# A transformer layer on one core: its first loads in halves, and the last of seven products added on in PSUM

## The chip, the cores and the metric

The kernel runs on one core of a Trainium2 chip. The core has a matrix engine (TensorE, PE in the profile; PEld is its weight load), a vector engine (VectorE, DVE), an activation engine (ScalarE, ACT), GpSimd (POOL), and SyncE (SP), whose queue issues all of this kernel's DMAs to 16 DMA engines. Products are accumulated in eight PSUM banks; everything else works in SBUF. The metric is the device time of one execution in microseconds; a median over runs is given.

## The reference, cut to what matters

One layer over 1024 rows of width 1024, in fp32:

```python
h = rmsnorm(x, g_mix_pre)
proj = h @ w_in                     # q, k, v of two groups of heads, and 8 forget-gate logits
y = concat(rmsnorm(forgetting_attention(...)), rmsnorm(chunked_attention(...)))
x = x + rmsnorm(y @ w_out, g_mix_post)
x = x + rmsnorm(memory_cross_attention(rmsnorm(x, g_mem_pre), ...), g_mem_post)
h = rmsnorm(x, g_ff_pre)
y = square(relu(h @ w_ff1)) @ w_ff2 # hidden width 4096
x = x + rmsnorm(y, g_ff_post)
```

## The kernel before

Every fp32 product is made as three products of rounded parts: an operand is split into a high part (a copy rounded to the type that PE takes) and a low part (the operand less its high part), and `mm3` (lines 191 to 195) multiplies high by high, high by low and low by high into one bank. So each operand costs a copy and a subtraction before PE can use it: mostly the copy on ACT and the subtraction on DVE.

**The start.** x comes transposed from the host (`xT`), 512 rows at a time (a half `th`), in four pairs of 128-row chunks of the width (`load_pair`, 512 KB each). The first work on PE are the values of the first 512 rows, block by block of 128 rows: group 1 (the chunked heads, 256 columns, weights `w_v1`) and group 0 (the forgetting heads with the gate's logits, 264 columns, `w_v0`). `value_weights` loads `w_v1` in two blocks of four chunks and `w_v0` in blocks of three, three and two; `value_split` splits them. `gained(kc)` multiplies a chunk of x by its gain and splits it (ACT writes `hT_hi`, DVE `hT_lo`). `square(kc)` squares a chunk on ACT and adds it up on DVE; the sum goes through PE (`ssx`) and POOL (a power of -0.5) to become the inverse norm of each row, `rcols[0]`. The other half's inverse norm, `rcols[1]`, comes from the rows of x themselves: four loads (`row`), four squares with a running sum on ACT (`row_squares`), POOL. While they wait for that, 30 transposes of the identity (`warm`) keep PE at work.

The order on every engine in this part, in the middle of the feed-forward layer and at the end is the order in which the code issues the instructions (`tc.manual_schedule()`); each engine works through its own in that order, and SP's queue too. Only the attention between them is ordered by a planner (`Flow`). A tile's `bufs` say how many buffers its tag has; a new tile waits until the one whose buffer it takes has been used for the last time. In the first stage PE goes through the eight chunks with four banks at once (96 products), then `ssx`, then the group-0 values of block 0 and block 1 (24 products each), then a transpose that spreads the inverse norms over the partitions (`rr`), and further values.

**The feed-forward layer.** Both matrix products are done by seven products of half-size blocks with added and subtracted operands (Strassen's scheme in Winograd's form). The first product's outputs `u`, `g` and `s` are combined on DVE (`sums`, lines 1974 to 1984) and written to DRAM (`put`). The second product takes its seven products in this order, each in eight steps of 24 products:

```python
order = ((0, "B11"), (1, "B21"), (4, "T2"), (3, "T1"), (5, "T3"), (6, "B22"), (2, "T4"))
```

`fetch(s)` loads the operands of step `s`, and `prepare(s)` (lines 1876 to 1905) makes the weight operand and splits both. Two sets of four banks are used: `X` and `Y`. B11 starts X; T2 and T3 are added on in the same banks; B21 and T1 start Y, B22 is added on to T1. `gather` (line 2044) takes a product's banks out into the output rows `yc`. Before, T4 starts fresh banks, and `gather` subtracts them from what T3 left.

**The end.** The last three steps of T4 are done block by block (`tp`), so that each block's rows can be finished beside the next: `gather`, `squares` (square with sum on ACT, gain on DVE), `inverse` (POOL), `finish` (DVE adds the residual, SP writes the result).

Of the kernel before, what the change touches and what calls it, by code (L numbers as in the profile page):

```python
# [14 lines left out]
F32 = mybir.dt.float32  # L15
# [7 lines left out]
P = 128  # L23
# [112 lines left out]
def build(ctx, tc, nc, out, t):  # L136
# [150 lines left out]
    def value_weights(g, raws=None, only=None):  # L287

        n = 264 if g == 0 else 256
        src = t["w_v0"] if g == 0 else t["w_v1"]  # L290
        raws = [] if raws is None else raws
        for i, (a, b) in enumerate(((0, 3), (3, 6), (6, 8)) if g == 0 else ((0, 4), (4, 8))):
            if only in (None, i):
                raw = wp.tile([P, b - a, n], F32, tag="wraw", bufs=3, name=f"wrawv{g}{a}")
                nc.sync.dma_start(raw, src[:, a:b, :])
                raws.append(raw)
        return raws

    def value_split(g, raw, i, pieces=1):
        k, shape = raw.shape[1], list(raw.shape)  # L300
        if g == 1:
            wh, wl = (wp.tile(shape, F32R, tag=x, bufs=2, name=f"{x}v{i}") for x in ("whi", "wlo"))
        else:
            wh, wl = (u4(f"{x}v0{i}", shape) for x in ("whi", "wlo"))
        n = k // pieces
        for j in range(0, k, n):
            nc.scalar.activation(wh[:, j:j + n, :], raw[:, j:j + n, :], AF.Copy)
            nc.vector.tensor_sub(wl[:, j:j + n, :], raw[:, j:j + n, :], f(wh[:, j:j + n, :]))
        return [(wh[:, j, :], wl[:, j, :]) for j in range(k)]
# [1060 lines left out]
    with tc.manual_schedule():  # L1370
        xT = {0: [load_pair(0, 0)], 1: []}
        gmix = const.tile([P, KC], F32, name="gmix")
        nc.sync.dma_start(gmix, t["g_mix_pre"])
        raw1 = value_weights(1, None, 0)
        xT[0] += [load_pair(0, 1), load_pair(0, 2)]
        value_weights(1, raw1, 1)
        xT[0].append(load_pair(0, 3))
        raw0 = value_weights(0, None, 0)
# [5 lines left out]
        def gained(kc):  # L1384

            x, g, dh = xT[0][kc // 2][:, kc % 2, :], gmix[:, kc:kc + 1], hT[0].hi(kc)
            nc.scalar.activation(dh, x, AF.Copy, scale=g)
            nc.vector.scalar_tensor_tensor(hT[0].lo(kc), x, g, f(dh), op0=ALU.mult, op1=ALU.subtract)
# [11 lines left out]
        for kc in (0, 1):  # L1400
            gained(kc)
        w1 += value_split(1, raw1[0], 0, 2)
# [26 lines left out]
        w0 += value_split(0, raw0[1], 1)  # L1429
        nc.vector.tensor_scalar(rcols[0], ps, EPS, None, op0=ALU.add)  # L1430
        nc.gpsimd.tensor_tensor(rcols[0], rcols[0], mhalf[:, 0:4], op=ALU.pow)
        w0 += value_split(0, raw0[2], 2)

        def row(b):
            xr.append(p1.tile([P, D], F32, tag="sp", bufs=5, name=f"x{b}"))
            nc.sync.dma_start(xr[-1], t["x"][b * P:(b + 1) * P, :])
# [439 lines left out]
    def prepare(s):  # L1876

        n, k = steps[s]
        name = order[n][1]
        ra = rows_a.pop(s)  # L1880
        if s % 3 == 2 or s == len(steps) - 1:
            ah, al, bh, bl = [u4(f"{m}{s}", (P, D)) for m in ("ah", "al", "bh", "bl")]
        else:
            ah, al = [wp.tile([P, D], F32R, tag=m, bufs=2, name=f"{m}f{s}") for m in ("whi", "wlo")]
            bh, bl = [pws[s % 3].tile([P, D], F32R, tag=f"v{s % 3}{m}", bufs=1, name=f"v{m}f{s}")
                          for m in ("hi", "lo")]
        rb = rows_b.pop(s)[0] if name not in ("B11", "T1") else None
# [10 lines left out]
        nc.scalar.activation(ah, ra, AF.Copy)  # L1898
        nc.scalar.activation(bh, rb, AF.Copy)
        nc.vector.tensor_sub(al, ra, f(ah))  # L1900
        nc.vector.tensor_sub(bl, rb, f(bh))
        if name == "B11":
            t1[k] = u4(f"t1_{k}", (P, D), F32)
            nc.vector.tensor_sub(t1[k], r12, rb)
        ops[s] = (ah, al, bh, bl)

    with manual:
# [79 lines left out]
        sums()  # L1987


        pfs.close()  # L1990
        yc, ssf = {}, {}

        def squares(b, nh, apart=False):

            y = yc[b][:, nh * HT:(nh + 1) * HT]
            if b not in ssf:
                ssf[b] = small.tile([P, 2], F32, tag="ssf", bufs=8, name=f"sf{b}")
            junk = pw.tile([P, HT], BF16, tag="sd", bufs=1, name=f"jf{b}{nh}")
            nc.scalar.activation(junk, y, AF.Square, scale=1.0 / 32.0, accum_out=ssf[b][:, nh:nh + 1])  # L1999
            g = yg[b, nh] = u4(f"yg{b}{nh}", (P, HT), F32) if apart else y  # L2000
            nc.vector.tensor_tensor(g, y, gfin[:, nh * HT:(nh + 1) * HT], op=ALU.mult)
# [42 lines left out]
        def gather(n, tp, ps):  # L2044
# [10 lines left out]
            elif n == 4:  # L2055
                nc.scalar.activation(half(hi, 0), ps, AF.Copy)
                nc.vector.tensor_add(half(hi, 1), ps, half(hi, 1))
            elif n == 5:
                nc.vector.tensor_add(half(lo, 1), ps, half(lo, 1))
            else:  # L2060
                nc.vector.tensor_sub(half(hi, 0), half(hi, 0), ps)
# [19 lines left out]
        for n in range(7):  # L2081
            if n in (0, 6):
# [5 lines left out]
            for k in range(NK - tail):  # L2088
                s = n * NK + k
                if s + 2 < len(steps):  # L2090
                    prepare(s + 2)
                if s + 4 == len(steps):
# [5 lines left out]
                multiply(banks, range(4), [s], n in (2, 4, 5))  # L2098
# [10 lines left out]
        for tp in range(4):  # L2109
            multiply(X, [tp], range(len(steps) - 3, len(steps)), False)  # L2110
# [9 lines left out]
def _layout(i):  # L2120
# [10 lines left out]
    def rows(w):  # L2131
        return a(w.reshape(KC, P, -1).transpose(1, 0, 2))
# [10 lines left out]
        "w_v0": rows(np.concatenate([fv[:, :256], fg], 1)),  # L2143
        "w_v1": rows(cv[:, :256]),
# [29 lines left out]
```

## Time and profile before

| what | value |
|---|---|
| median of 3 runs | 1483.99 us (1483.71 to 1484.88) |
| profiled execution | 1484.06 us, its span 1482.3 us |
| PE busy | 1466.0 us, 99% of the span |
| DVE busy | 948.6 us, 64% |
| ACT busy | 797.3 us, 54% |
| POOL busy | 391.3 us, 26% |
| moved by DMA | 220.67 MB, mean 149 GB/s |
| granted PE clock, mean | 0.999 |

The profile is that of one execution. The span runs from the first to the last recorded instruction; the time of the execution is a little longer. A row of a timeline gives start, duration, engine, line of the kernel, operation, output and inputs, shapes, how many instructions are merged (x2), and in brackets how long the engine had been idle before and what released it. Line numbers are those of the kernel before. A wait list names who waited, for whom, and how long in total, how often, and the longest. Rows of PE overlap, as products are pipelined: the distance between two starts is what one costs.

### The profile page before, as it was taken

The numbers are of one execution on the slowest core, as the hardware profiler recorded it, in microseconds if no ns is written. First come the engines' busy times: TensorE is split into PE (matmuls) and PEld (weight loads), VectorE is DVE, ScalarE is ACT, GpSimd is POOL, SyncE is SP. The second block draws the span as 40 slices with busy tenths as digits, with TensorE's granted clock in tenths as the row PEclk, the third lists the DMA queues.
The fourth block names the chain that finished last, engine by engine and source line by source line (L and its number), as shares of the span: only waits on it lengthen the run. The fifth ranks groups of instructions, "written<-read, shape, count | busy, mean of one in ns | idle before, by whom it ended". The sixth has DMA issues, their size and how long they took to land. (4 is left out here: it accounts for less than half of the span.)

```text
span 1482.3 us, 21601 instructions
## 1 busy us (share of the span) xinstructions
PE 1466.0 (99%) x7606; PEld 1250.3 (84%) x7606; DVE 948.6 (64%) x1644; ACT 797.3 (54%) x1417; POOL 391.3 (26%) x613
## 2 busy tenths in 40 slices
PE   8999999999999999999999999999999999999998
PEld 8989888888889988888888887888888888888886
DVE  6777667565576835974384687675444665656577
ACT  6567567465567835553353455555555453443542
POOL 0144355353344200531041413432222000000021
PEclk9999999999999999999999999999999999999999
DMA  7133322522315552461251447674445785445565
GB/s 271 48 87 79 82 67 70 150 67 60 79 58 149 176 178 85 154 202 58 89 182 43 153 146 241 235 243 148 155 150 170 250 346 178 142 139 202 178 247 199
DMA packets 83484, 220.67 MB, mean 149 GB/s; under 512 B 10008, under 2 KB 14112, under 8 KB 83376
## 3 DMA queue, kind: packets, MB, share of 16 engines
q1 hardware_dynamic: 83376, 219.30, 44.6%
q8 instruction: 60, 0.98, 0.3%
q14 instruction: 48, 0.39, 0.1%
HBM read 159.96 MB, written 50.91 MB: 142 GB/s over the span
## 5 line engine op out<-in xcount | busy, mean ns | idle before, releaser
L700 DVE TENSOR_TENSOR pl<-ptr,ph 128x512 fp32r<-128x512 f32 (+1 forms) x152 | 92.2, 616 | 39.5 <-ACT ph L703 34.8
L1898 ACT ACTIVATE whif<-ra 128x1024 fp32r<-128x1024 f32 x37 | 39.2, 1061 | 122.1 <-PE fy L194 62.6
L1900 DVE TENSOR_TENSOR wlof<-ra,whif 128x1024 fp32r<-128x1024 f32 x37 | 45.3, 1225 | 91.2 <-ACT whif L1898 91.2
L703 ACT ACTIVATE ph<-ptr 128x512 fp32r<-128x512 f32 (+1 forms) x152 | 79.1, 539 | 39.4 <-PE ptr L694 32.9
L2014 POOL TENSOR_SCALAR rf<-sf 128x1 f32<-128x1 f32 x8 | 8.2, 1028 | 326.6 <-ACT jf L1999 326.3
L731 PE MATMUL pv<-ph,vs 128*128 128x256 f32 x304 | 79.6, 286 | 0.0
L732 PE MATMUL pv<-pl,vs 128*128 128x256 f32 x304 | 78.6, 283 | 0.3 <-DVE pl L700 0.3
L193 PE MATMUL fx<-vhif,whif 128*128 128x512 f32 x168 | 65.4, 389 | 0.0
L194 PE MATMUL fx<-vlof,whif 128*128 128x512 f32 x168 | 65.4, 389 | 0.0
L195 PE MATMUL fx<-vhif,wlof 128*128 128x512 f32 x168 | 65.4, 389 | 0.0
L732 PEld LDWEIGHTS pv<-pl,vs 128*128 128x128 f32 x304 | 57.6, 189 | 4.6 <-POOL pl L689 0.5
L731 PEld LDWEIGHTS pv<-ph,vs 128*128 128x128 f32 x304 | 57.3, 189 | 4.1
L1788 POOL TENSOR_TENSOR sc<-wf,wf 128x512 f32<-128x512 f32 x14 | 20.1, 1437 | 144.0 <-DMA wf<-in_w_ff 89.3
L193 PE MATMUL k<-hT_hi,whik 128*128 128x512 f32 x128 | 52.5, 411 | 0.0
L193 PE MATMUL mq<-h2T_hi,whimq 128*128 128x512 f32 x128 | 51.5, 403 | 0.0
L193 PE MATMUL q<-hT_hi,whiq 128*128 128x512 f32 x128 | 50.9, 398 | 0.0
L193 PE MATMUL ym<-whimo,oT_hi 128*128 128x512 f32 x128 | 50.3, 394 | 0.1
L194 PE MATMUL k<-hT_lo,whik 128*128 128x512 f32 x128 | 50.2, 393 | 0.0
L193 PE MATMUL yw<-whiwo,yT_hi 128*128 128x512 f32 x128 | 50.2, 392 | 0.0
L195 PE MATMUL k<-hT_hi,wlok 128*128 128x512 f32 x128 | 50.1, 392 | 0.0
L194 PE MATMUL q<-hT_lo,whiq 128*128 128x512 f32 x128 | 50.1, 391 | 0.0
L195 PE MATMUL mq<-h2T_hi,wlomq 128*128 128x512 f32 x128 | 50.1, 391 | 0.0
(606 smaller groups left out, 5027.1 us busy)
## 6 DMA issues: line engine op xcount, KB each, us to landing
ra<-gd SPq DMA_DIRECT2D x56, 512.0 KB, 3.9
wg<-in_w_ff SPq DMA_DIRECT2D x56, 512.0 KB, 5.9
wf<-in_w_ff SPq DMA_DIRECT2D x38, 512.0 KB, 4.0
gd<-s SPq DMA_DIRECT2D x48, 256.0 KB, 2.1
wrawmq<-in_w_mq SPq DMA_DIRECT2D x16, 512.0 KB, 3.8
wrawmo<-in_w_mo SPq DMA_DIRECT2D x16, 512.0 KB, 3.8
gd<-u SPq DMA_DIRECT2D x32, 256.0 KB, 2.1
gd<-g SPq DMA_DIRECT2D x25, 256.0 KB, 2.5
```

The source lines that it names most:

```text
L193: nc.tensor.matmul(ps, lh, rh, start=start, stop=False, skip_group_check=more)
L194: nc.tensor.matmul(ps, lh, rl, start=False, stop=False, skip_group_check=more)
L195: nc.tensor.matmul(ps, ll, rh, start=False, stop=stop, skip_group_check=more)
L700: flow.put("V", at, 0.7, lambda: nc.vector.tensor_sub(pl[:, live, :], tr[:, live, :], f(ph[:, live, :])), done)
L703: flow.put("S", flow.end, 0.6, lambda ph=ph, tr=tr, live=live: nc.scalar.activation(ph[:, live, :], tr[:, live, :], AF.Copy), split)
L731: nc.tensor.matmul(pv, v, ph[:, hs, :], start=c == 0 and half == 0, stop=False)
L732: nc.tensor.matmul(pv, v, pl[:, hs, :], start=False, stop=c + 1 == len(steps) and half == 1)
L1788: eng.tensor_sub(sc[:, k1], r0[:, k0], r1[:, k0])
L1898: nc.scalar.activation(ah, ra, AF.Copy)
L1900: nc.vector.tensor_sub(al, ra, f(ah))
L2014: nc.gpsimd.tensor_scalar(r, ssf[b][:, 0:1], ssf[b][:, 1:2], EPS, op0=ALU.add, op1=ALU.add)
```

## The change

It has three parts.

1. The start. A tiny activation (`early`) is issued first on ACT. The first pair of x and the first block of `w_v1` are loaded in two halves each, in the order x, gmix, weights, x, weights. `w_v0` and `w_v1` are laid out by block in DRAM, so that a block is contiguous. The high part of the first block of `w_v1` is copied by POOL instead of ACT, and its low part goes ahead of the low parts of x on DVE. There are 20 warm-up transposes instead of 30. The second block of `w_v0` gets a buffer of another tag (`bias`) and is loaded and split sooner; two of the four rows of x are loaded ahead of the third block; the values of group 0, block 0 are issued before `ssx`; all four `row_squares` go ahead of `value_leave`.
2. Between the two feed-forward products: `prepare(2)` to `prepare(4)` are issued ahead of the last `sums()`, with its four writes to DRAM, instead of behind it.
3. The end: T4's operand is made with the opposite sign, and its products are added on in X, in the banks in which T3 ended. The copies of half of X after T3 and the four subtractions of `gather` go; `squares` reads the bank itself, on ACT and DVE.

```diff
-    def load_pair(th, p):
+    def load_pair(th, p, halves=False):
...
-        nc.sync.dma_start(xt, t["xT"][th, p])
-        return xt
+        if not halves:
+            nc.sync.dma_start(xt, t["xT"][th, p])
+            return xt
+        return xt, [lambda j=j: nc.sync.dma_start(xt[:, j, :], t["xT"][th, p][:, j, :]) for j in (0, 1)]
...
+    VPARTS = {1: ((0, 4), (4, 8)), 0: ((0, 3), (3, 6), (6, 8))}
+
+    def value_raw(g, i, tag=None, halves=False):
+        n, (a, b) = 264 if g == 0 else 256, VPARTS[g][i]
+        shape = [P, b - a, n]
+        raw = (wp.tile(shape, F32, tag="wraw", bufs=3, name=f"wrawv{g}{a}") if tag is None else
+               p1.tile(shape, F32, tag=tag, bufs=2, name=f"wrawv{g}{a}"))
+        src = t[f"w_v{g}"][a * P * n:b * P * n].rearrange("(p k n) -> p k n", p=P, n=n)
+        if not halves:
+            nc.sync.dma_start(raw, src)
+            return raw
+        h = (b - a) // 2
+        return raw, [lambda j=j: nc.sync.dma_start(raw[:, j:j + h, :], src[:, j:j + h, :]) for j in (0, h)]
+
+    def value_split(g, raw, i, pieces=1, between=None):
...
-            nc.scalar.activation(wh[:, j:j + n, :], raw[:, j:j + n, :], AF.Copy)
+            if between:
+                nc.gpsimd.tensor_copy(wh[:, j:j + n, :], raw[:, j:j + n, :])
+            else:
+                nc.scalar.activation(wh[:, j:j + n, :], raw[:, j:j + n, :], AF.Copy)
             nc.vector.tensor_sub(wl[:, j:j + n, :], raw[:, j:j + n, :], f(wh[:, j:j + n, :]))
+            if between and j == 0:
+                between()
...
-        xT = {0: [load_pair(0, 0)], 1: []}
+        early = const.tile([P, 1], F32, name="early")
+        nc.scalar.activation(early, mhalf[:, 0:1], AF.Copy)
+        xt, xloads = load_pair(0, 0, True)
+        raw, wloads = value_raw(1, 0, halves=True)
+        xT, raw1 = {0: [xt], 1: []}, [raw]
         gmix = const.tile([P, KC], F32, name="gmix")
+        xloads[0]()
         nc.sync.dma_start(gmix, t["g_mix_pre"])
-        raw1 = value_weights(1, None, 0)
+        wloads[0]()
+        xloads[1]()
+        wloads[1]()
...
-        for n in range(30):
+        for n in range(20):
...
-        for kc in (0, 1):
-            gained(kc)
-        w1 += value_split(1, raw1[0], 0, 2)
+        gained_hi(0)
+        w1 += value_split(1, raw1[0], 0, 2, lambda: (gained_lo(0), gained(1)))
...
-        value_weights(0, raw0, 1)
-        value_weights(0, raw0, 2)
+        raw0 += [value_raw(0, 1, "bias"), None]
         for kc in (4, 5):
             square(kc)
         w0 += value_split(0, raw0[0], 0)
+        w0 += value_split(0, raw0[1], 1)
         for kc in (6, 7):
             square(kc)
+        for b in (4, 5):
+            row(b)
+        raw0[2] = value_raw(0, 2)
+        w0 += value_split(0, raw0[2], 2)
+        ps0 = [values(0, w0, 0, "s")]
...
-        for b in range(4, TB):
+        for b in (6, 7):
             row(b)
         for p in range(4):
             xT[1].append(load_pair(1, p))
-        ps0 = [values(0, w0, 0, "s")]
-        for b in (4, 5):
+        for b in (4, 5, 6):
             row_squares(b)
+        row_squares(7)
         for kb in range(4):
             value_leave(1, kb, first[kb])
-        for b in (6, 7):
-            row_squares(b)
...
-        elif name in ("T3", "T4"):
+        elif name == "T3":
             nc.vector.tensor_sub(rb, t2b[k], rb)
+        elif name == "T4":
+            nc.vector.tensor_sub(rb, rb, t2b[k])
...
-        sums()
-        pfs.close()
+        prepare(2)
...
-        def squares(b, nh, apart=False):
-            y = yc[b][:, nh * HT:(nh + 1) * HT]
+        def squares(b, nh, bank=None):
+            y = yc[b][:, nh * HT:(nh + 1) * HT] if bank is None else bank
...
             elif n == 4:
-                nc.scalar.activation(half(hi, 0), ps, AF.Copy)
                 nc.vector.tensor_add(half(hi, 1), ps, half(hi, 1))
-            elif n == 5:
+            else:
                 nc.vector.tensor_add(half(lo, 1), ps, half(lo, 1))
-            else:
-                nc.vector.tensor_sub(half(hi, 0), half(hi, 0), ps)
...
-            if n in (0, 6):
+            if n == 0:
                 X = four(f"fx{n}", ("mm", "s"))
...
-                if s + 2 < len(steps):
+                if 0 < s < len(steps) - 2:
                     prepare(s + 2)
+                if s == 2:
+                    sums()
+                    pfs.close()
...
-                multiply(banks, range(4), [s], n in (2, 4, 5))
+                multiply(banks, range(4), [s], n in (2, 4, 5, 6))
...
-            gather(6, tp, X[tp])
-            squares(tp + 4, 0, True)
+            squares(tp + 4, 0, X[tp])
             inverse(tp + 4)
```

More of the change, by code (lines that the diff above doesn't have):

```diff
@@ L1999, in squares @@
             nc.scalar.activation(junk, y, AF.Square, scale=1.0 / 32.0, accum_out=ssf[b][:, nh:nh + 1])
-            g = yg[b, nh] = u4(f"yg{b}{nh}", (P, HT), F32) if apart else y
+            g = yg[b, nh] = y if bank is None else u4(f"yg{b}{nh}", (P, HT), F32)
             nc.vector.tensor_tensor(g, y, gfin[:, nh * HT:(nh + 1) * HT], op=ALU.mult)
@@ L2109, in build @@
         for tp in range(4):
-            multiply(X, [tp], range(len(steps) - 3, len(steps)), False)
+            multiply(X, [tp], range(len(steps) - 3, len(steps)), True)
             if tp:
                 finish(tp + 3)
-            gather(6, tp, X[tp])
-            squares(tp + 4, 0, True)
+            squares(tp + 4, 0, X[tp])
             inverse(tp + 4)
@@ L2129, in blocks, with parts @@
         return a(w.reshape(KC, P, -1, P).transpose(2, 1, 0, 3))
-    def rows(w):
-        return a(w.reshape(KC, P, -1).transpose(1, 0, 2))
+    def parts(w, ranges):
+        w = w.reshape(KC, P, -1)
+        return a(np.concatenate([w[x:y].transpose(1, 0, 2).reshape(-1) for x, y in ranges]))
     w = i["w_in"][0]
@@ L2142, in _layout @@
         "w_qk": blocks(np.concatenate([fq, fk, cq, ck], 1)),
-        "w_v0": rows(np.concatenate([fv[:, :256], fg], 1)),
-        "w_v1": rows(cv[:, :256]),
+        "w_v0": parts(np.concatenate([fv[:, :256], fg], 1), ((0, 3), (3, 6), (6, 8))),
+        "w_v1": parts(cv[:, :256], ((0, 4), (4, 8))),
         "w_v": blocks(np.concatenate([fv[:, 256:], cv[:, 256:]], 1)),
```

35 lines of the change are left out of this document (13 added, 22 removed).

## The prediction

> **What bounds the kernel now.** I read the head of the page first, then who TensorE (PE) waited for, then the timeline of each engine around the three places that the change touches.
>
> ```profile
> span 1482.3 us, 21601 instructions
> PE 1466.0 (99%) x7606; PEld 1250.3 (84%) x7606; DVE 948.6 (64%) x1644; ACT 797.3 (54%) x1417; POOL 391.3 (26%) x613
> ...
> PE v L193 <- ACT whiv L307: 2.7, 1, 2.7
> PE rr L1464 <- POOL rx L1456: 1.0, 1, 1.0
> PE fx L194 <- DVE bl L1901: 0.7, 1, 0.7
> ```
>
> PE is busy for 1466.0 of 1482.3 us, and the change leaves its products as they are. So time can only come from the 16.3 us in which PE stands: before the first product, in the few waits of this list, and behind the last product. The change touches all three. The profiled execution took 1484.06 us, 1.76 beside its span and 0.07 above the median of the runs (1483.99), so I reckon from 1484.06 and take 0.07 off at the end. A measurement of this kernel can tell about 0.2% (2.97 us) from no change.
>
> **The start, before.** Timelines of ACT, DVE, PE and POOL (start, duration, engine, line, operation):
>
> ```profile
> 4.50 1.28 ACT L1387 ACT_TABLE_LOAD   x1 [4.50 <-DMA gmix<-in_g_mix_pre]
> ...
> 8.57 1.15 ACT L307 ACTIVATE whiv<-wrawv 128x512 fp32r<-128x512 f32 x2 [1.45 <-DMA wrawv<-in_w_v]
> 9.87 1.34 ACT L1387 ACTIVATE hT_hi<-xT,gmix 128x512 fp32r<-128x512 f32 x2
> ...
> 20.22 1.39 ACT L307 ACTIVATE whiv<-wrawv 128x792 fp32r<-128x792 f32 x2
> ...
> 22.54 1.04 ACT L1442 ACTIVATE junk<-x 128x1024 bf16<-128x1024 f32 x1
> ...
> 32.05 1.29 ACT L1472 ACTIVATE hT_hi<-xT 128x512 fp32r<-128x512 f32 x2 [0.33 <-DVE xT L1471]
> ```
>
> ```profile
> 10.63 1.41 DVE L1388 SCALAR_TENSOR_TENSOR hT_lo<-xT,gmix,hT_hi 128x512 fp32r<-128x512 f32 x2
> ...
> 14.23 1.29 DVE L308 TENSOR_TENSOR wlov<-wrawv,whiv 128x512 fp32r<-128x512 f32 x2
> ...
> 19.56 0.98 DVE L308 TENSOR_TENSOR wlov<-wrawv,whiv 128x792 fp32r<-128x792 f32 x1
> 20.45 1.48 DVE L1397 TENSOR_TENSOR sqx<-sqx,sqx 128x512 f32<-128x512 f32 x2
> ...
> 23.16 0.71 DVE L308 TENSOR_TENSOR wlov<-wrawv,whiv 128x528 fp32r<-128x528 f32 x1
> ```
>
> ```profile
> 9.98 0.39 PE L194 MATMUL v<-wlov,hT_hi 128*128 128x256 f32 x1 [0.34 <-DVE wlov L308]
> ...
> 21.36 0.28 PE L195 MATMUL v<-whiv,hT_lo 128*128 128x256 f32 x1
> 21.99 1.05 PE L1428 MATMUL ssx<-o,sqx 128*128 128x1 f32 x8 [0.35 <-DVE sqx L1397]
> 22.90 0.37 PE L193 MATMUL v<-whiv,hT_hi 128*128 128x264 f32 x1
> ...
> 28.68 0.28 PE L195 MATMUL v<-whiv,hT_lo 128*128 128x264 f32 x1
> 29.95 1.09 PE L1464 MATMUL rr<-ident,rx 128*128 128x128 f32 x8 [0.99 <-POOL rx L1456]
> ...
> 36.69 0.28 PE L193 MATMUL v<-whiv,hT_hi 128*128 128x256 f32 x1
> ```
>
> ```profile
> 23.33 1.43 POOL L1431 TENSOR_TENSOR rx<-rx,mhalf 128x4 f32<-128x4 f32 x1 [22.04 <-DVE rx L1430]
> 28.53 0.24 POOL L1455 TENSOR_SCALAR rx<-ssx 128x4 f32<-128x4 f32 x1 [3.77 <-ACT junk L1442]
> ```
>
> The first four value banks take 96 products, the second at 9.98 and the 96th at 21.36: 0.121 us each. The two blocks of 24 with 264 columns (22.90 to 28.68) go at 0.123. Three things stand ahead of 9.98: the table load, which sits behind the landing of gmix, the 512 KB of weights that land just before 8.57, and the splitting.
>
> **The start, changed, part by part.** The table load moves to the kernel's first microsecond, where ACT has nothing else: 1.28 us off the path. The first weights come as two halves, and their high part is copied by POOL. Before has no POOL copy of 128x512; the nearest rows lie on both sides:
>
> ```profile
> L436 POOL TENSOR_TENSOR wloq<-wrawq,whiq 128x512 fp32r<-128x512 f32 x16 | 20.6, 1308 | 34.6 <-ACT whiq L427 34.5
> ...
> L632 POOL TENSOR_SCALAR spc2g<-spc2g,smc2g 128x640 f32<-128x640 f32 x4 | 3.2, 799 | 3.9 <-DVE smc2g L631 3.9
> ```
>
> I take 0.8, by the row with one tensor input. The first half lands between gmix (4.50) and the whole block before (8.57); I take 6.2, about the middle. Then POOL to 7.0, and on DVE, in its order, the low weights (0.65) and the low x (0.71), which queues behind the wait for POOL: the third product, and with it the stream, runs from 8.4 instead of about 10.1. But it cannot keep that. The next pair of x arrives behind the same megabyte as before, so I leave it at 9.87, and from there ACT and DVE do the same work in the same order up to 19.56: low x of the third chunk done at 10.63 + 0.75 = 11.38, low weights of the fifth at 14.23 + 0.69 = 14.92. By that wait the fifth chunk's second product (number 50) goes at 14.95, and product 96 at 14.95 + 46 x 0.121 = 20.5, 0.85 earlier. A first half as late as 7.0, or POOL at 1.31, costs nothing here; at 8.57 it would cost 0.8.
>
> Behind it the order changes. The second block of the other weights has a buffer of its own and no longer waits for one, and its low part goes ahead of two additions on DVE: 19.56, 20.45, then the additions (1.4) to 22.8, then the last low part (0.71) to 23.5. The block of 24 that starts at 20.6 needs that one at its 20th product: it stalls some 0.6 and ends at 24.1. The sums of squares (ssx), moved behind this block, hold PE 0.91, so the second block runs 25.0 to 28.1. Their result goes to POOL: 24.1 + 1.05, 0.3 through DVE, 1.43, to 26.9. The other rstd queues behind that on POOL: its sums on ACT need four rows of 1.04 from 22.1, when the additions free a buffer (ACT's copies were done at 21.6 even before), so 26.3; POOL starts at 26.95 and, as from 28.53 to 29.95, PE gets it 1.42 later, at 28.4. Against 29.95 that is **1.6 us**. The four rows of x are issued ahead of where they were, so they have landed by then. It is kept: hT of the other half is there at 32.05 + 0.65 for a use at 36.69, and its chain moves up too.
>
> **The middle.**
>
> ```profile
> 1178.14 1.06 ACT L1898 ACTIVATE whif<-ra 128x1024 fp32r<-128x1024 f32 x1 [0.45 <-DMA ra<-gd]
> ...
> 1175.83 0.69 DVE L1977 TENSOR_TENSOR s<-u,g 128x512 f32<-128x512 f32 x1 [1.36 <-ACT u L1604]
> ...
> 1179.63 1.22 DVE L1901 TENSOR_TENSOR bl<-wg,bh 128x1024 fp32r<-128x1024 f32 x1
> ...
> 1180.90 0.50 PE L194 MATMUL fx<-bl,ah 128*128 128x512 f32 x1 [0.73 <-DVE bl L1901]
> ```
>
> The third step of the second feed-forward matrix waited 0.73 for its low part, which stood behind the last sums of the first matrix on DVE. The change puts its preparation ahead of them: the four sums of 0.69 hold DVE from 1175.83 to about 1178.5, so bl can come up to 2.7 us earlier, where 0.73 is needed, and the stall goes. Late next would be the fourth step, whose operand lands at 1178.14 and which is 24 products further on: no stall. The sums and their four DRAM writes now queue behind the fifth step's preparation on ACT, DVE and SP's queue; the first reader of what they write is the last step of the third product, some 20 steps on. **0.73 us**.
>
> **The end.**
>
> ```profile
> 1474.61 0.39 PE L195 MATMUL fx<-bh,al 128*128 128x512 f32 x1
> ...
> 1475.04 0.69 DVE L2061 TENSOR_TENSOR yc<-yc,fx 128x512 f32<-128x512 f32 x1
> ...
> 1475.82 0.63 ACT L1999 ACTIVATE jf<-yc 128x512 bf16<-128x512 f32 x1 [3.36 <-DVE yc L2061]
> ...
> 1477.62 0.75 DVE L2021 SCALAR_TENSOR_TENSOR xf<-yg,rf,xf 128x512 f32<-128x512 f32 x1 [1.17 <-POOL rf L2015]
> ```
>
> The sum is now made in PSUM (the operand is negated where it is prepared, at the same price), so the subtraction at 1475.04 goes and ACT squares the bank itself, 0.04 behind the product: 1475.82 - 1475.04 = **0.78 us**. New is that DVE's gain product waits for ACT, since both read the bank; DVE had 1.17 idle there, and the wait takes 0.8 of it. The four copies to SBUF that go elsewhere were hidden beside the eight steps of the next product, and so save nothing.
>
> Sum: 1.6 + 0.73 + 0.78 = 3.1. 1484.06 - 3.1 - 0.07 = **1480.9**.
>
> **The rivals.** All hang on when the second pair of x lands, since the start moves with it one for one.
>
> The queue's early hole closes. The rate of the DMA engines in the first 48 us, in slices of 1.2:
>
> ```profile
> GB/s 0 65 374 261 184 317 348 420 427 406 374 98 26 51 313 364 345 348 335 403 393 345 331 109 328 137 345 410 399 113 3 0 7 0 7 0 0 0 0 0
> ```
>
> Slices four and five move 261 and 184 where the third had 374, so (113 + 190) x 1.2 / 374 = 1.0 us is lost while the strided weights come in. They are contiguous now, and more is queued early. Against it: the second block had the same stride and came in the slices at over 400. Gain 4.1: 1479.9; I let the range go to twice that shift, 2 us, 1478.9. (By the same line 3.8 MB are in at 13; the two rows of x that now go ahead of the last weights on SP's queue put those at 5.3 MB, some 4 us later, near 17, for a use at 20.5: hidden.)
>
> Halves cost a fixed part. Stores of both sizes:
>
> ```profile
> x1d<-xtw SPq DMA_DIRECT2D x8, 512.0 KB, 2.6
> ...
> out_y<-xf SPq DMA_DIRECT2D x16, 256.0 KB, 2.1
> ```
>
> 256 KB more take 0.5, so 1.6 of a transfer is fixed. If one such part is not overlapped, x lands 1.6 later, the start's gain is gone, and 1482.5 is left. The Trainium skill (DMA: Bandwidth & Descriptors, Bandwidth) says to batch transfers to 1 MiB or more, which speaks against halves; by its fixed cost of about 2.0 us, paid for both added transfers, the sum would be +0.9, 1484.9. The trace so far speaks against paying it in a row: the pair of x landed 1.3 us behind the weights (8.57 to 9.87), bytes and all.
>
> Slower: the start of the queue goes by transfers and not by bytes. The 128 rows of the first weights took from gmix's landing (4.50) to 8.57, 4.1 us. If each of the two added transfers holds the queue as long, x moves by 8.2 and the result to 1480.9 + 8.2 = 1489.1; from a shift of 3.1 on the kernel is slower than before. Against it speaks the same 1.3 us between the two landings.
>
> The array runs slow. 20 warm-up transposes instead of 30 (transposes in a stretch, third number):
>
> ```profile
> 4.30:4.80 0.50, 0.50 (x4) 0.50 (x3) 1.00 0.88 254
> 4.80:5.30 0.50, 0.50 (x7) 0.50 (x6) 1.00 0.81 221
> ```
>
> Up to about 4.8 they take twice as long as after it. At some 0.22 and then 0.11 each, 20 of them end near 5.3, just past the switch. Should the first 24 products go at half speed, 0.242, the stream from 8.4 reaches the third chunk at 13.7 rather than 11.4 and the 20th product of the next block at 24.5 instead of 23.5: at most 1.0, 1481.9. The Trainium skill (TensorE: Matmul & The Clock Gate, Part 1) has the clock rise after some 3.4 us of sustained work in a window that runs freely, and fall after as long an idle one; the trace agrees that it rises in the course of the warm-up, at 4.8, and by the second rule the 2 us of idle here would pass.
>
> **How the numbers follow.** Forecast, x within half a microsecond of 9.87: 0.44, of which 0.28 lies over 0.2%, since 3.1 is near the bound of 2.97. Hole closes: 0.30, all faster. Fixed part: 0.13, and slow array: 0.05, both within 0.2%. By transfers: 0.08, slower. So faster 0.58, same 0.34, slower 0.08. The range goes from the 2 us of the second case, 1478.9, to a little past the fixed part, 1482.9; what it leaves out is the slower case and the edges.
>
> **What would show it.** In the changed profile: the table load near 1 us; the PE list without bl and with wlov waits of 0.5 to 1 in the first 25 us; rr at 28.4 with little wait; ACT's square 0.04 behind the last product. ACT's second pair of hT_hi is the test: at 9.9 the sum holds, at 8 to 9 it is better, beyond 13 the kernel is slower. A bl wait of 0.7 elsewhere near the start of the second feed-forward matrix, or a first product after 9, would prove a step wrong.

## The result, and the profile after

The changed kernel takes 1479.54 us (median; 1478.87 to 1480.52, seven runs), the kernel before, run beside it, 1484.85 (1483.66 to 1485.26, seven runs): a ratio of 0.9965, 95% interval 0.9955 to 0.9975. That is 5.3 us less; the forecast was 3.1 less, and 1480.9. Of the 2.2 between the two, 0.9 is the base: the forecast started from the earlier median of 1483.99. The profiled execution, 1480.52 us, is the slowest of the seven, and one wait near 470 us belongs to it alone (below).

The head of the page and the list of whom PE waited for (total, times, longest):

```profile
span 1478.7 us, 21579 instructions
PE 1466.6 (99%) x7596; PEld 1249.7 (85%) x7596; DVE 948.0 (64%) x1640; ACT 795.6 (54%) x1412; POOL 394.7 (27%) x615
...
PE v L194 <- DVE wlov L317: 1.1, 3, 0.5
PE pz L193 <- DVE g L1976: 0.7, 1, 0.7
PE ptr L705 <- POOL spc6g L643: 0.5, 1, 0.5
PE v L195 <- DVE hT_lo L1422: 0.5, 2, 0.3
```

PE is as busy as before (1466.6 against 1466.0), and the span is 3.6 shorter: only standing time went. The 2.7 ahead of the first product, the 1.0 at `rr` and the 0.7 at `bl` are gone from the list. What replaces them in the start are small waits for low parts from DVE.

Timelines of ACT, POOL and PE in the start (start, duration, engine, line, operation, idle time before and its releaser):

```profile
0.72 1.28 ACT L1383 ACT_TABLE_LOAD   x1 [0.72 <-PEq L2194]
...
5.56 0.72 ACT L1419 ACTIVATE hT_hi<-xT,gmix 128x512 fp32r<-128x512 f32 x1 [1.26 <-DMA xT<-in_xT]
9.02 1.34 ACT L1419 ACTIVATE hT_hi<-xT,gmix 128x512 fp32r<-128x512 f32 x2 [2.74 <-DMA xT<-in_xT]
...
4.91 0.61 POOL L314 CAST whiv<-wrawv 128x512 fp32r<-128x512 f32 x1 [3.62 <-DMA wrawv<-in_w_v]
24.61 1.03 POOL L1463 TENSOR_TENSOR rx<-rx,mhalf 128x4 f32<-128x4 f32 x1 [16.19 <-DVE rx L1462]
...
26.06 1.05 POOL L1481 TENSOR_TENSOR rx<-rx,mhalf 128x4 f32<-128x4 f32 x1
...
6.96 0.39 PE L195 MATMUL v<-whiv,hT_lo 128*128 128x256 f32 x1 [0.28 <-DVE hT_lo L1422]
14.13 0.39 PE L194 MATMUL v<-wlov,hT_hi 128*128 128x256 f32 x1 [0.53 <-DVE wlov L317]
22.66 0.39 PE L194 MATMUL v<-wlov,hT_hi 128*128 128x264 f32 x1 [0.35 <-DVE wlov L317]
23.38 0.95 PE L1461 MATMUL ssx<-o,sqx 128*128 128x1 f32 x8
27.17 1.08 PE L1489 MATMUL rr<-ident,rx 128*128 128x128 f32 x8
```

The second pair of x is there at 9.02 (9.87 before), product 50 goes at 14.13 (forecast 14.95), `ssx` at 23.38 (24.1), `rr` at 27.17 (28.4; before 29.95). So the start gave 2.78 and not 1.6. `rr` waits for nothing now, but only just: POOL's last power, which it needs, ends at 27.11, and the products ahead of it leave PE at 27.17.

The end, one timeline of all engines:

```profile
1471.98 0.39 PE L195 MATMUL fx<-bh,al 128*128 128x512 f32 x1
1472.46 0.60 ACT L2026 ACTIVATE jf<-fx 128x512 bf16<-128x512 f32 x1 [3.39 <-PE fx L195]
...
1473.18 0.69 DVE L2028 TENSOR_TENSOR yg<-fx,gfin 128x512 f32<-128x512 f32 x1 [1.61 <-ACT jf L2026]
...
1474.23 0.75 DVE L2048 SCALAR_TENSOR_TENSOR xf<-yg,rf,xf 128x512 f32<-128x512 f32 x1 [0.35 <-POOL rf L2042]
```

From the last product to DVE's next-to-last step are 2.25, where before there were 1477.62 - 1474.61 = 3.01: 0.76 less. The gain product on DVE does wait for ACT, and still leaves 0.35 idle of the 1.17 that stood there.

### The profile page after: what moved, and what is told of

It is laid out like the page before. It is cut to its first block, busy times and chain, and to the rows that moved or that the text cites. A ratio compares the mean times of both kernels' runs of the same rounds, so it can differ in the third digit from the quotient of the medians.

```text
span 1478.7 us, 21579 instructions
## 1 busy us (share of the span) xinstructions
PE 1466.6 (99%) x7596; PEld 1249.7 (85%) x7596; DVE 948.0 (64%) x1640; ACT 795.6 (54%) x1412; POOL 394.7 (27%) x615
## 5 line engine op out<-in xcount | busy, mean ns | idle before, releaser
L194 PE MATMUL mq<-h2T_lo,whimq 128*128 128x512 f32 x128 | 50.1, 391 | 0.0
```

The lines of the kernel that those rows point to most:

```text
L194: nc.tensor.matmul(ps, lh, rl, start=False, stop=False, skip_group_check=more)
```

## The experiments

All times are medians; the kernel before was run beside each group (1484.60, 1484.69 and 1484.98).

**The parts alone.** `e1_start` is the changed kernel with the middle and the end as before; `e2_midend` is the kernel before with the middle and the end changed; `e4_again` is the changed kernel as it is.

```
e1_start:   if s + 2 < len(steps): prepare(s + 2)   # sums() ahead of all, T4 in fresh banks
e2_midend:  prepare(2); ... if s == 2: sums()       # T4 on top of T3, start as before
```

> Only the first part of the change (the start); the middle and the end as before. Theory A: the three parts add up as the traces show them, and the start is worth the 2.8 us by which the transposes rr come earlier (29.95 to 27.17). Then 1484.9 - 2.8 = about 1482.1, ratio 0.998, with the waits for bl (0.7) and the subtraction at the end back in the profile. Rival B: the start's lead is given back on the way (the changed profile lost 0.75 us of it near 470 us, behind a late landing of a key weight of the memory), so that 2.0 us or less is left at the end, and the rest of the 5.3 us comes from the other two parts. In the trace: A has the last product 2.5 to 2.9 us earlier than before, B 2.0 or less.

> Only the second and the third part (preparations ahead of the last sums; the last product added on in PSUM); the start as before. Theory A: 0.73 for the wait of bl and 0.8 to 1.0 for the subtraction behind the last product, 1.5 to 1.8 in all, so about 1483.2, ratio 0.999. Rival B: these two carry most of the measured 5.3 us, that is 2.5 or more, ratio 0.998 or less. In the trace: no wait for bl, ACT's square 0.04 behind the last product, first product at 9.3 as before.

> The changed kernel itself once more, for its time on the same chip and in the same rounds as the others, and for a second trace. Theory A: the wait of 0.54 for POOL near 470 us was a late landing in that one execution and is not there again, or elsewhere; the last product is 3.3 to 3.6 us earlier than before and the time near 1479.5. Rival B: it is there again, since the lead of the start runs into a load that cannot come earlier; the last product is 2.6 us earlier again.

| kernel | time | ratio to before, interval |
|---|---|---|
| `e1_start` | 1482.38 | 0.9987 (0.9978 to 0.9996) |
| `e2_midend` | 1482.37 | 0.9986 (0.9978 to 0.9995) |
| `e4_again` | 1479.37 | 0.9965 (0.9952 to 0.9977) |

By the medians the start alone brings 2.2, the middle and the end together 2.2, and all three 5.2, more than the 4.4 of the sum. The trace of `e1_start` fits its theory A, with the last product 3.0 earlier than before, but it is of the fastest run; the median lies between the theories. So does that of `e2_midend`.

`e4_again` has no wait at 470; its `rr` is at 26.77 and its last product at 1470.74, 3.87 ahead of before. In the trace of after that wait comes from one load of key weights that landed 7.2 us after its issue. Here is its row, the rows of `e4_again`, and then the clock in `e2_midend` (a stretch, its length, busy time of PE, PEld, DVE, ACT and POOL, granted PE clock, DMA share, GB/s):

```profile
469.77 0.55 PE L705 MATMUL ptr<-ident,spc6g 128*128 128x128 f32 x3 [0.54 <-POOL spc6g L643]
```

```profile
26.77 1.07 PE L1489 MATMUL rr<-ident,rx 128*128 128x128 f32 x8
...
1470.74 0.39 PE L195 MATMUL fx<-bh,al 128*128 128x512 f32 x1
```

```profile
PE v L193 <- ACT whiv L307: 2.8, 1, 2.8
...
11.00:11.40 0.40, 0.40 (x6) 0.40 (x5) 0.40 (x2) 0.40 (x2) 0.00 (x0) 1.00 1.04 421
11.40:14.80 3.40, 3.40 (x19) 3.40 (x18) 3.16 (x6) 3.40 (x7) 0.00 (x0) 0.50 0.70 273
...
30.80 1.09 PE L1464 MATMUL rr<-ident,rx 128*128 128x128 f32 x8 [1.00 <-POOL rx L1456]
```

This I had not reckoned with: two microseconds after PE's products begin, its clock is halved for 3.4 us. Products go at 0.214 there instead of 0.12, and `rr` comes at 30.80 instead of the 29.95 of the profile before, with the same start in the code. So in the traces the middle and the end are worth more than the 1.5 expected: their last product is 0.24 earlier than before although `rr` is 0.85 later, and the chain behind it shorter.

**Whole loads.** `e3_wholes` is the changed kernel without the halves.

```diff
-        xt, xloads = load_pair(0, 0, True)
-        raw, wloads = value_raw(1, 0, halves=True)
+        xt = load_pair(0, 0)
...
-        wloads[0]()
-        xloads[1]()
-        wloads[1]()
+        raw = value_raw(1, 0)
```

> The changed kernel with the first pair of x and the first block of weights loaded whole again, in the order x, gmix, weights; all else as changed. Theory A: the halves bring the first products, not the second pair of x, which comes behind the same bytes and lands near 9.0 as in the changed kernel. The weights land near 7.7, POOL, low weights and low x follow, the third product runs near 9.9 instead of 6.96; most of that goes into waits that follow anyway, and rr comes some 0.7 us later (27.8): about 1480.2. Rival B: the halves also bring the second pair of x earlier; with whole loads it lands at 9.9 again and rr at 28.4 or later, 1.3 us or more slower than the changed kernel.

It took 1482.46 (0.9985, 0.9976 to 0.9994), 3.0 over the changed kernel. Yet the second pair of x is as early, and that was the test of B:

```profile
8.97 1.34 ACT L1415 ACTIVATE hT_hi<-xT,gmix 128x512 fp32r<-128x512 f32 x2 [3.08 <-DMA xT<-in_xT]
...
PE v L193 <- POOL whiv L314: 2.5, 1, 2.5
...
29.50 0.75 PE L1485 MATMUL rr<-ident,rx 128*128 128x128 f32 x5
...
11.00:11.40 0.40, 0.40 (x4) 0.40 (x4) 0.40 (x2) 0.40 (x2) 0.00 (x0) 0.50 1.06 423
```

Neither theory holds: the pair comes with A, the time with B. PE stands 2.5 ahead of its first product, as before the change, and its clock is halved from 9.75 to 13.1; `rr` goes only at 29.50. The next three kernels take these apart.

**The layout, the idle, and whole loads with the idle filled.**

```diff
 e5_contig   (kernel before; w_v0 and w_v1 laid out block by block)
-                nc.sync.dma_start(raw, src[:, a:b, :])
+                nc.sync.dma_start(raw, src[a * P * n:b * P * n].rearrange("(p k n) -> p k n", p=P, n=n))
...
 f1_warm54   (kernel before)
-        for n in range(30):
+        for n in range(54):
 f2_wholes43 (e3_wholes)
-        for n in range(20):
+        for n in range(43):
```

> The kernel before, with nothing changed but the value weights laid out block by block in DRAM. Three kernels with that layout (the changed one twice, and the one with whole loads) had ACT's second pair of hT_hi at 8.6 to 9.0, those without at 9.84 and 9.87. Theory A: the strided rows made the early hole in the DMA queue, and the layout closes it: the pair of x is there at 9.0 or earlier, the first weights before 8.0 instead of 8.57, rr about 0.8 earlier than 29.95, the time about 0.8 below the kernel before beside it. Theory B: the hole was closed by something else (the order of the loads, more queued early): the pair stays at 9.85, rr at 29.95, the time is that of the kernel before.

> The kernel before with 54 warm-up transposes instead of 30, so that PE has work until about 9.0, where it stood 2.7 us ahead of its first product. Its products and their data come no earlier. In several traces the granted clock is 0.5 for one stretch of 3.4 us shortly after such a stand (11.4 to 14.8 in the kernel with the middle and the end alone, 9.75 to 13.1 in the one with whole loads), and runs of the kernel before lie between 1482.7 at a mean clock of 0.999 and 1486.5 at 0.996. Theory A: the idle ahead of the first product lets the clock fall in part of the executions: filled with work, all runs have 0.999 or more, the median is 1483.4 and none is over 1484.6. Theory B: the falls come by chance or by load and not from the idle: the median stays at 1484.6 with runs up to 1486.5 and clocks of 0.996 and 0.997 among them.

> The changed kernel with whole first loads (median 1482.46, mostly at a clock of 0.997) and 43 warm-up transposes instead of 20, so that PE has work until its first product at 8.4. Theory A: of the 3.0 us that whole loads cost, half is the halved clock that their longer idle brings: with the idle filled the median is 1480.9 (1480.5 to 1481.3), the clock 0.999, and the rest, about 1.5 over the changed kernel's 1479.4, is the later start of the products. Theory B: all of the 3.0 is the later data: 1482.4 as before, whatever the clock. Theory C: all is the clock: 1479.5.

| kernel | time | ratio to before, interval |
|---|---|---|
| `e5_contig` | 1482.84 | 0.9986 (0.9976 to 0.9995) |
| `f1_warm54` | 1483.74 | 0.9994 (0.9985 to 1.0003) |
| `f2_wholes43` | 1480.18 | 0.9973 (0.9962 to 0.9984) |

`e5_contig`, in ACT's and PE's timelines and the DMA rate (GB/s in slices of 1.2 us):

```profile
7.71 1.15 ACT L307 ACTIVATE whiv<-wrawv 128x512 fp32r<-128x512 f32 x2 [0.50 <-DMA wrawv<-in_w_v]
9.00 1.34 ACT L1387 ACTIVATE hT_hi<-xT,gmix 128x512 fp32r<-128x512 f32 x2
...
29.08 1.09 PE L1464 MATMUL rr<-ident,rx 128*128 128x128 f32 x8 [1.00 <-POOL rx L1456]
...
GB/s 0 89 340 271 205 355 393 420 424 402 353 50 14 211 134 376 413 416 423 420 403 307 205 283 179 269 294 396 256 72 0 7 0 7 0 0 0 0 0 14
```

The weights land 0.86 earlier, x at 9.00, and `rr` goes 0.87 earlier: what theory A said. But slices four and five still move 271 and 205: the hole is not closed. And the same strided layout landed both sooner still in one execution of another kernel (`g3_end`, below), and the contiguous one put x at 9.70 in another (`g1_order`); the landing varies by over a microsecond between executions. What varies is the slowest of a load's 16 landing signals: for the first weights the first signal comes at 5.2 to 5.4 in the kernel before, in `e5_contig` and in `g3_end` alike, the last at 8.6, 7.7 and 6.4. The median of the ten executions is 1.9 below the kernel before, and not the 0.8 of theory A; none of them has a mean clock under 0.998, and against the executions of the kernel before at 0.999 (below) they lie 0.8 lower. The layout's share is likely, and it is not settled by one trace.

`f1_warm54`: with PE at work to its first product, none of 11 executions had a mean clock under 0.998; five had 0.998, where theory A wanted 0.999. Of the 71 executions of the kernel before beside all the groups, 32 had 0.997 or less, with a mean of 1485.3 us, and 22 had 0.999, with a mean of 1483.6. The median fell by 0.95, towards the 1483.4 that theory A gave, though two executions lie over its 1484.6, and the interval just holds no change. The warm-ups keep the clock up; they don't bring the data sooner.

`f2_wholes43` is the clearer one. Whole loads without the idle cost 0.7 over the changed kernel and not 3.0, by the medians: 2.3 us of what the halves bring is the idle, and 0.7 the earlier data (its `rr` is 0.8 to 1.2 later than in the changed kernel). The intervals of the two overlap, so the 0.7 is not shown by the times alone:

```profile
3.75 5.12 PE L1396 MATMUL warm<-ident 128*128 128x128 f32 x32
...
27.95 1.08 PE L1485 MATMUL rr<-ident,rx 128*128 128x128 f32 x8
```

The median lies about midway between theories A (1480.9) and C (1479.5). The traces show 1.55 of the 2.3: `rr` goes at 27.95 instead of 29.50. That is what a halved stretch costs a PE that is never idle in it, 16 products at 0.214 instead of 0.12, 1.5 us. No trace shows where the other 0.75 comes from.

**Additions on POOL.**

```diff
-                nc.vector.tensor_add(sq[0], sq[0], sq[kc])
+                nc.gpsimd.tensor_add(sq[0], sq[0], sq[kc])
```

> The changed kernel with the seven additions of the squares on POOL instead of DVE. Theory A: the waits that are left in the start (0.3 to 0.5 at product 50, 0.35 at the 20th product of the next block) hang on DVE's order alone: they go, rr comes 0.5 to 0.9 earlier than 26.8 to 27.2, the median is about 1478.7. Theory B: POOL takes 1.3 for each addition, so that the last ends after 24 and ssx and the row sums behind it on POOL come later: a wait at ssx or rr of 0.5 to 1.5, and a median of 1479.5 to 1480.5.

It took 1482.44 (0.9986, 0.9977 to 0.9994), 3 us more than the changed kernel, and worse than both theories. Timelines of DVE and POOL, and PE's wait list:

```profile
19.23 5.76 DVE L317 TENSOR_TENSOR wlov<-wrawv,whiv 128x792 fp32r<-128x792 f32 x3
...
13.94 10.49 POOL L1409 TENSOR_TENSOR sqx<-sqx,sqx 128x512 f32<-128x512 f32 x6 [1.55 <-ACT sqx L1407]
...
PE v L194 <- DVE wlov L317: 1.4, 3, 0.6
...
29.56 0.63 PE L1489 MATMUL rr<-ident,rx 128*128 128x128 f32 x4
```

POOL is busy for 10.1 of these 10.49 us: 1.68 for an addition, and not 1.30 as the first one took, beside which DVE stood for part of the time. Two of DVE's two-input subtractions of 128x512 beside them take 2.39 instead of 1.29. So the last low weights are ready at 24.99 (19.23 + 5.76) and not at 22.60 as in the changed kernel, where the additions are on DVE. The Trainium skill (GPSIMD Engine Reference, Specifications) says that POOL reaches SBUF over an interface shared with DVE, with contention where a DVE instruction has two SBUF inputs; the trace agrees.

**The order on DVE, the table load, the end, and a second look at the start.** `g1_order` issues the squares and additions behind the weights' low parts; `g2_notable` leaves the first activation away; `g3_end` is the kernel before with the end alone; `e1_look` is `e1_start` once more.

```diff
 g1_order (changed kernel)
-        for kc in (0, 1):
-            square(kc)
         for kc in (4, 5):
             gained(kc)
         w1 += value_split(1, raw1[1], 1, 2)
-        for kc in (2, 3):
+        for kc in (0, 1, 2, 3):
             square(kc)
...
 g2_notable (changed kernel)
-        early = const.tile([P, 1], F32, name="early")
-        nc.scalar.activation(early, mhalf[:, 0:1], AF.Copy)
 g3_end (kernel before)
...
-                multiply(banks, range(4), [s], n in (2, 4, 5))
+                multiply(banks, range(4), [s], n in (2, 4, 5, 6))
...
```

> The changed kernel with another order in the start, all work on the engines it was on: the squares of the first two chunks and their addition behind the splitting of the second block of weights, the squares of the last two behind the splitting of the last block, and one buffer for what the row squares throw away, so that ACT doesn't wait for DVE's additions before them. Theory A: the two waits for low weights that are left (0.31 to 0.53 at product 50, 0.35 at the 20th product of the next block) hang on the additions ahead of them on DVE: they go, ssx starts at 22.3 to 22.7 instead of 23.0 to 23.4, rr at 26.1 to 26.5 instead of 26.8 to 27.2, and the median is 0.6 lower than the changed kernel's 1479.4 to 1479.5, so 1478.8. Theory B: rr is held by POOL (the power of ssx at 24.6, then 0.24 and 1.05 for the rows), and what PE gains it waits there: rr stays at 26.8 to 27.2, the median at 1479.4.

> The changed kernel without the tiny first activation, so that ACT loads its table behind the landing of gmix again. Theory A: the load's 1.28 us delay the first products (the third goes at about 8.3 instead of 7.0 to 7.5), but the wait at product 50, which DVE's order and the second pair of x set, takes that up: rr within 0.3 of 26.8 to 27.2; what it costs is at most a halved clock through the longer idle: median 1479.4 to 1480.5. Theory B: the load is on the path with all its 1.28: rr at 28.1 to 28.4, median 1480.7.

> The kernel before with the end alone: the last product added on in the banks of T3. The middle and the end together gave 2.2 us where 1.5 was expected. Theory A: the end is worth the subtraction, 0.78 from the last product to the last instruction, and no more: 0.8 below the kernel before beside it. Theory B: taking four copies of 128x512 from ACT and the subtractions from DVE also ends waits further ahead: 1.5 or more below, with the last product earlier against rr than before.

> The start alone once more, for a second trace. Its median (1482.4) is 3.0 over the changed kernel's, though the middle and the end that it lacks are worth 1.5 in the traces; its one trace so far was of its fastest run (1480.9). Theory A: in most of its runs the clock is halved for 3.4 us at a place where the products are not waiting for data, or twice: a time of 1482 or more with a granted clock of 0.5 behind 14 us, and rr at 28 or later. Theory B: the clock has no part in it: no second stretch of 0.5, rr at 27, and the difference lies behind the start.

| kernel | time | ratio to before, interval |
|---|---|---|
| `g1_order` | 1479.17 | 0.9962 (0.9949 to 0.9976) |
| `g2_notable` | 1478.79 | 0.9962 (0.9950 to 0.9975) |
| `g3_end` | 1483.09 | 0.9987 (0.9979 to 0.9996) |
| `e1_look` (one run) | 1480.78 | |

`g1_order`, ACT and PE:

```profile
9.70 2.63 ACT L1419 ACTIVATE hT_hi<-xT,gmix 128x512 fp32r<-128x512 f32 x4 [1.80 <-DMA xT<-in_xT]
...
27.33 1.09 PE L1488 MATMUL rr<-ident,rx 128*128 128x128 f32 x8
```

In this execution x landed 0.7 to 1.1 later than in the changed kernel's two traces, and `rr` is only 0.2 to 0.6 later: the reordering may well bring its half microsecond, but one trace with another landing doesn't show it, and the medians differ by 0.2 to 0.4 inside the spread of both. The two waits for low weights are gone, as theory A said, but `ssx` now waits for the last addition on DVE and starts at 23.37. What the order is worth stays open.

`g2_notable`, ACT, PE:

```profile
3.59 1.28 ACT L1417 ACT_TABLE_LOAD   x1 [3.59 <-DMA gmix<-in_g_mix_pre]
4.89 0.72 ACT L1417 ACTIVATE hT_hi<-xT,gmix 128x512 fp32r<-128x512 f32 x1
...
6.98 0.39 PE L195 MATMUL v<-whiv,hT_lo 128*128 128x256 f32 x1 [0.28 <-DVE hT_lo L1420]
...
26.88 1.08 PE L1487 MATMUL rr<-ident,rx 128*128 128x128 f32 x8
```

Without the early table load the third product goes at 6.98, as with it (6.96), and `rr` at 26.88. The load lies beside the weights' landing, POOL's copy and DVE's subtraction, and not on the path. Theory A holds, and below its range: 1478.79, the lowest median of all. With intervals that cover each other it is not shown to be faster than the changed kernel; it shows that one part of the change brings nothing.

`g3_end`, ACT's row of the second pair of x and the end:

```profile
8.16 1.32 ACT L1387 ACTIVATE hT_hi<-xT,gmix 128x512 fp32r<-128x512 f32 x2
...
1472.75 0.39 PE L195 MATMUL fx<-bh,al 128*128 128x512 f32 x1
1473.23 0.60 ACT L2002 ACTIVATE jf<-fx 128x512 bf16<-128x512 f32 x1 [3.39 <-PE fx L195]
```

The profiled execution of this kernel, with the start as before, had both first loads in before ACT could use them, so that PE stood 0.7 and not 2.7; it was the fastest of its kernel (1481.41). From the first product of the second feed-forward matrix (1167.0) to the last it takes 305.75, before 1474.61 - 1168.9 = 305.71: the copies and subtractions that went had cost no time in between. Behind the last product its span has 1479.6 - 1472.75 = 6.85 left, before 1482.3 - 1474.61 = 7.69. So the end is worth 0.84 in the trace: theory A. The median is 1.9 lower with an interval of 0.6 to 3.1, which is too wide to tell the theories apart.

`e1_look` again was one of the quick ones: no halved clock, `rr` at 27.01, 1480.78. Its trace fits theory B's first half, but both traces of the start alone (1480.89 and 1480.78) are some 1.5 below that kernel's median. What its slower executions had, no trace shows, and their mean clocks do not either: of the eight from 1482.1 up, five had 0.999 and three 0.998.

## Why the prediction was right, and where it was not

**The start: right in its steps, too small by 1.2 to 1.6.** It gave 2.78 and 3.18 in the two traces of the changed kernel. Two terms were mis-sized. The step that failed is "I leave it at 9.87": x came at 9.02 and 8.64, with product 50 at 14.13 instead of 14.95 and `ssx` 0.72 ahead of the forecast. And the power on POOL, taken as 1.43 from the row of before, took 1.03: before, DVE was subtracting two operands beside it (its row at 23.16), now DVE stands, and `e8_pooladds` shows what the two do to each other. In all five traces with the old order in the start this power took 1.43, in the nine others 1.03. Smaller: POOL's copy took 0.61 (0.8 taken), its half landed at 4.9 and 5.5 (6.2 taken), and the stall at the block's 20th product was 0.35 (0.6 taken). The waits for low weights came where they were placed.

**"1.28 us off the path" was wrong.** `g2_notable` shows nothing of it. The sum didn't use it, as it went by the second pair of x; the sentence should have asked what else ends at the same time. In the kernel before, too, ACT was done with the first pair of x and idle for 1.45 when the weights landed at 8.57.

**The middle.** The wait for `bl` is gone, and nothing stalls later. From the first product of that matrix to the last, `e2_midend` takes 304.67 (1474.37 - 1169.7) and `e4_again` 304.64 (1470.74 - 1166.1), before 305.71: about 1.05, of which the list shows 0.73. All of it lies at that one stop, since a list of waits counts only the time after the last product has run out. These are the products around it before (the one at 1180.90 stands between them):

```profile
1179.79 0.39 PE L193 MATMUL fx<-bh,ah 128*128 128x512 f32 x1
...
1181.24 0.40 PE L195 MATMUL fx<-bh,al 128*128 128x512 f32 x1
```

From start to start the two steps take 1.11 and 0.34, where others take 0.23: 0.88 and 0.11 lost. **The end** is 0.76 in the chain and 0.84 in the span, 0.78 forecast.

With these the traces give 3.18 + 1.05 + 0.84 = 5.1 for `e4_again`, less 0.4 that it gives back between `rr` (3.18 ahead) and the feed-forward matrix (2.8 ahead): 4.7, and its span is 4.8 shorter than before. In the trace of after only 1.6 of the start's 2.78 is left at that matrix, most of the loss at the wait near 470. That its span is 3.6 shorter, close to the 3.1 of the sum, is therefore luck: a start that gave more and a late load nearly cancel.

**The rivals.** The one with the early hole gave 1479.9 and came nearest, and its sign (x at 8 to 9) was what was seen; its mechanism was not, and that its number came near is luck: the slices that it wanted filled move 290 and 217 in the changed kernel, against 261 and 184 before:

```profile
GB/s 0 131 205 290 217 333 398 420 410 421 389 409 389 397 406 389 410 99 14 89 345 297 266 336 326 403 416 167 7 0 0 7 0 0 0 0 0 0 14 0
```

What closed is the other hole, at 13 to 17. Halves with a fixed part, and a queue that goes by transfers, fell: x came earlier and not later, with two transfers more ahead of it. The Trainium skill (DMA: Bandwidth & Descriptors, Bandwidth) asks for batches of 1 MiB or more; here whole loads of 512 KB did not gain, `f2_wholes43` being 0.7 slower by its median.

**The clock, with the sign turned.** The prediction feared half speed through ten warm-ups less in the changed kernel. Its two traces don't have it, by a small margin: the clock rose at 5.9 and 5.3, and the warm-ups ended at 5.9 and 5.6. `e8_pooladds`, which has the same first products, does have it. There the clock rose only at 10.8:

```profile
7.63 0.42 PE L193 MATMUL v<-whiv,hT_hi 128*128 128x256 f32 x1
7.85 0.42 PE L194 MATMUL v<-wlov,hT_hi 128*128 128x256 f32 x1
...
10.82 0.28 PE L193 MATMUL v<-whiv,hT_hi 128*128 128x256 f32 x1
10.94 0.28 PE L194 MATMUL v<-wlov,hT_hi 128*128 128x256 f32 x1
```

So whether that rival comes true can differ between executions with the same first products. Product 50 went at 14.53 there, 0.4 to 0.8 behind the changed kernel's; how much of that would be left at `rr` without the additions on POOL, no run shows. The profile gives this stretch a granted clock of 1.00, as it does for all time ahead of the first rise, so the mean of 0.999 or more that all 12 executions of the changed kernel had says nothing of a late rise.

What the mean can show is a fall behind the rise, and there it is the kernel before that seems to pay. `e2_midend`, with the same start, has 3.4 us at half clock behind its idle of 2.8. For the kernel before itself this is inferred from the mean clocks; its one trace has no such stretch. The mean also counts a fall behind the last product, which every trace has (at 1479.4 in the profile before). At a mean clock of 0.999 the kernel before takes 1483.6 and the changed one 1479.5: 4.1 of the 5.3. The other 1.2 fits the executions with a lower mean, of which no trace was kept.

## What to carry to other kernels

Ask of idle time ahead of the first products not only how long it is, but what the array's clock does after it: work that fills the gap can buy time though the data come no sooner, as the 2.3 us of `f2_wholes43` did. Before a step is moved off the path, look for what else ends at the same moment; the table load cost nothing because the weights were there no sooner (in `g2_notable` the load ends at 4.87, and POOL's copy of them starts at 4.92). And a sum made from one execution should say which of its rows vary between executions: in the three traces with the start of the kernel before, unchanged, `rr` goes at 28.23, 29.95 and 30.80, and the edit moved it by 2.8 to 3.2.

## What the runs showed of the hardware

Where a trace has a halved clock behind the rise, it begins late and lasts the same 3.4 us: 11.4 to 14.8 in `e2_midend` (idle 6.4 to 9.2), 9.75 to 13.1 in `e3_wholes` (idle 5.9 to 8.4), and 8.1 to 11.5 in `e1_start`, whose waits were 0.62, 0.34 and 0.28 only:

```profile
8.10:11.50 3.40, 3.40 (x19) 3.40 (x18) 2.29 (x4) 2.59 (x5) 0.37 (x1) 0.51 1.02 416
...
27.05 1.07 PE L1489 MATMUL rr<-ident,rx 128*128 128x128 f32 x8
```

There it cost next to nothing. Product 50 went at 14.60 without a wait, where the changed kernel's waited 0.53 and 0.31 for its low weights and went at 14.13 and 13.74; and the wait at the next block's 20th product (0.35 there) is gone too, so that `rr` is as early as without. The profile before has the same idle as `e2_midend` and no halved clock: it is not the length of the idle alone. The Trainium skill (TensorE: Matmul & The Clock Gate, Part 1) has a window of about 3.4 us that runs freely: the trace agrees with its length. It has the clock fall after a whole idle window; here it fell after 2.8, 2.5 and even 1.2 us of idle, and the measurement decides.
